# The head of a two-layer decoder kernel: other order of transfers, squares summed ahead of one product by ones, row factors multiplied partly on POOL

## The chip, the cores and the metric

One core of a Trainium2 chip runs the whole program. The metric is the time of one execution in microseconds (us), the median of several runs on the device.

## The reference

Two decoder layers over 512 tokens of width 1024, each of which also attends into 256 fixed memory tokens. What the change touches is only the beginning: the memory and the input are normed by their root mean square, and the memory is multiplied by the key and value weights of both layers.

```python
def rms_norm(x, g):
    xf = x.astype(jnp.float32)
    y = xf * lax.rsqrt(jnp.mean(xf * xf, axis=-1, keepdims=True) + EPS)
    return (y * g.astype(jnp.float32)).astype(x.dtype)

mem_n = rms_norm(mem, ln_mem)                 # 256 memory tokens
for layer in range(DEPTH):                    # two layers
    h = rms_norm(x, ln_mix[layer])
    mkv = mem_n @ w_mem_kv[layer]             # keys, then values, 256 columns each
    mem_k, mem_v = mkv[..., :MEM_W], mkv[..., MEM_W:]
    if layer < N_A_LAYERS:
        mix_out, mem_q = gated_deltanet_mixer(h, gdn_w_in[a], ...)   # begins with h @ w_in
    ...
```

## The kernel before, in words

All activations lie with the features on the 128 partitions. The input `x` has eight rows of tiles (k = 0 to 7, each 128 features by 512 tokens), the memory `mem` eight rows of 128 by 256. Products are made in three parts: each factor is split into a rounded high part and the rest (`whi` and `wlo` of a weight, `h` and `l` of `x`, `mh` and `ml` of `mem`), and high by high, low by high and high by low are summed in PSUM by `mm3`. The high part is an ACT copy (`copy`, L148), the rest a DVE subtraction (`split`, L161, or with a gain in it `split_gain`, L164).

The head of the program is `mem_and_norm` and `gates`. Its work in the order of the code:

- transfers, all issued by SP: gains, `mem` in four pieces with the first key weight in two halves between them, the second key weight, the constants, `x` in four pieces, the value weights, `wab`, and layer 1's key and value weights;
- the split of the eight rows of `mem`;
- `keys(0)`: two tiles of 24 matmuls each (PE, `pj<-mh,whi` and the like), without the norm's factor;
- `memory_stats` and `rstd_of`: the squares of `mem` on ACT (L151), summed by twos on DVE (`sq<-sq,sq`), and four products by a matrix of ones that sum over the partitions (`g<-sq,consts`); the factor `mr` from an ACT logarithm and an exponential (L142); the same with eight squares and four products for `x`, factor `xr`;
- `memory_columns`: `mr` as a column `mc`, by four small records on PE; `values(0)`, then `keys(1)` and `values(1)` (48 matmuls each);
- `norm()`: per row of `x`, DVE multiplies by the gain and by `xr` (L164, `x<-x,gains,xr`), ACT copies it to `h`, DVE subtracts to `l`;
- `gates`: eight products of `x`'s rows by `wab` (`pj<-x,wab`), their sum is copied by ACT to `ab`, and products by a constant matrix turn it (`g<-consts,ab`). The first projection `key(0)` of the next part begins directly behind the eight products on PE, and `g<-consts,ab` stands four matmuls into it.

Which engine does a step is written in the code. The order on each engine is set by a scheduler that works ahead of the run from priorities and estimates of its own; each engine then runs its list strictly in that order, and an instruction that waits holds up all behind it.

Of the kernel before, what the change touches and what calls it, by code (L numbers as in the profile page):

```python
# [9 lines left out]
F32 = mybir.dt.float32  # L10
# [3 lines left out]
ALU = mybir.AluOpType  # L14
# [4 lines left out]
P = 128  # L19
T = 512  # L20
D = 1024
KD = D // P
# [3 lines left out]
ML = 256  # L26
# [13 lines left out]
G_MIX, G_FFN, G_MEM, G_KV, G_FIN = (0, 8), (16, 24), 32, 40, 48  # L40
# [4 lines left out]

C_ID, C_U, C_ONE, C_CAUS, C_BAND = 0, 128, 256, 384, 512
C_SEL, C_INV, C_SIGN = 768, 780, 781
C_N = 782

# [19 lines left out]
def constants():  # L69
    c = np.zeros((P, C_N), np.float32)  # L70
    i = np.arange(P)
    c[:, C_ID:C_ID + P] = np.eye(P)
    c[:, C_U:C_U + P] = i[:, None] <= i[None, :]
    c[:, C_ONE:C_ONE + P] = 1.0
    c[:, C_CAUS:C_CAUS + P] = np.where(i[None, :] >= i[:, None], 0.0, NEG)
    c[:, C_BAND:C_BAND + P] = np.where(i[None, :] > i[:, None], 0.0, NEG)
    c[:, C_BAND + P:C_BAND + 2 * P] = np.where(i[None, :] <= i[:, None], 0.0, NEG)
    for e in range(12):
        c[e, C_SEL + e] = 1.0
        for j in range(1, 4):  # L80
            c[32 * j + e, C_SEL + e] = 1.0
    for p in range(P):
        if p % 64 < 16:
            c[p, C_INV] = INV_FREQ[p % 8]
            c[p, C_SIGN] = -1.0 if p % 64 < 8 else 1.0
    return c


class Builder:
# [138 lines left out]

    def rstd_of(self, tiles, pool, out, after=None):

        ps = self.bank("g")[:, :tiles[0].shape[1]]
        for k in range(0, KD, 2):
            two = []
            for x in tiles[k:k + 2]:
                sq = self.t(pool, [P, x.shape[1]], F32, "sq", 6)
                two.append(sq)
                ins = self.square(sq, x)
                if after is not None:
                    self.nosync(ins, after)
            self.tt(self.nc.vector, two[0], two[0], two[1], ALU.add)  # L240
            self.mm(ps, self.ones, two[0], k == 0, k == KD - 2)
        self.rsqrt(out, ps, D)


    def build(self):
# [32 lines left out]
    def load_constants(self, cp):  # L278
        nc, a = self.nc, self.a
# [6 lines left out]
        self.U = c[:, C_U:C_U + P]  # L286
        self.ones = c[:, C_ONE:C_ONE + P]
        self.caus = c[:, C_CAUS:C_CAUS + P]
        self.band = c[:, C_BAND:C_BAND + 2 * P]
        self.one = c[:, C_ONE:C_ONE + 1]  # L290
        v = self.t(cp, [P, 10], F32, "eps")
# [12 lines left out]
    def mem_and_norm(self, ep):  # L304
# [7 lines left out]
        early = lambda src: self.load(src, ep, 6)  # L312
        raw = [self.t(ep, [P, D], F32, "wraw", 6)]
        for k in range(0, KD, 2):
            nc.sync.dma_start(mem[:, k:k + 2, :], a["memT"][:, k:k + 2, :])
            if k < 4:
                s = slice(k // 2 * T, (k // 2 + 1) * T)
                nc.sync.dma_start(raw[0][:, s], a["wmk"][0, 0][:, s])
        raw += [early(a["wmk"][0, 1])]
        self.fetch_constants()  # L320
        for k in range(KD):
            self.split_gain(mem[:, k, :], self.gain(G_MEM, k), mh[:, k, :], ml[:, k, :])
        for k in range(0, KD, 2):
            nc.sync.dma_start(x[:, k:k + 2, :], a["xT"][:, k:k + 2, :])
        raw += [early(s) for s in (a["wmv"][0, 0], a["wmv"][0, 1])]
        wab = self.wab = self.t(ep, [P, KD, 32], F32, "wab")
        nc.gpsimd.memset(wab, 0.0)
        nc.sync.dma_start(wab[:, :, 0:12], a["wab"])
        raw += [early(s) for s in (a["wmk"][1, 0], a["wmk"][1, 1], a["wmv"][1, 0], a["wmv"][1, 1])]
        self.kept = {}  # L330
        mr = self.t(ep, [P, ML], F32, "mr")
        mc = self.t(ep, [P, 2], F32, "mc")
        xr = self.t(ep, [P, T], F32, "xr")
        mem_stats = lambda after: self.memory_stats(ep, mem, mr, after)

        def keys(layer):
            ps, ks = [], []
            for m in range(2):
                w = self.weight(None, nc.vector, raw[4 * layer + m], 1 if m + layer else 2)
                ps.append(self.bank("sc" if layer else "pj")[:, :ML])  # L340
                for k in range(KD):
                    self.mm3(ps[m], w, k, (mh[:, k, :], ml[:, k, :]), k == 0, k == KD - 1)
            if layer == 0:
                mem_stats(self.copied)
            for m in range(2):
# [26 lines left out]
        def norm():  # L372
            self.h, self.hx = [], [x[:, k, :] for k in range(KD)]
            for k in range(KD):
                self.h.append(self.pair(self.apool))
                xk = x[:, k, :]
                self.stt(xk, xk, self.gain(G_MIX[0], k), xr, ALU.mult, ALU.mult)
                self.split(xk, *self.h[k])

        self.memK = keys(0)  # L380
        self.rstd_of([x[:, k, :] for k in range(KD)], ep, xr)
        self.memory_columns(mr, mc)
        self.memV = values(0)
        keys(1)
        values(1)
        norm()

    def memory_stats(self, ep, mem, mr, after):
        self.rstd_of([mem[:, k, :] for k in range(KD)], ep, mr, after=after)

# [900 lines left out]
```

## Time and profile before

| what | value |
|---|---|
| median of 3 runs | 1148.49 us (1147.78 to 1148.76) |
| the profiled execution's own time | 1148.39 us |
| its span, first to last instruction | 1146.6 us |
| share of the span: PE, DVE, ACT, POOL | 98%, 73%, 55%, 7% |
| chain that ended last | PE 89%, DVE 5%, ACT 4%, DMA 1%, issue 1% |
| the eight products of the gates begin / end on PE | 40.53 us / about 42.4 us |

The head is the first 42 us of the span. In a row of the timeline the first number is the start, the second the duration (of all x instructions together), and in brackets stands how long the engine had been idle before, and what ended that. A row of a table by stages gives the stretch, its length, and for each engine the busy time and the number of instructions. In a row of groups the number behind the bar is the busy time of the group and then the mean duration of one instruction in ns.

### The profile page before, as it was taken

How to read it: one execution, taken by the hardware profiler on the slowest of the kernel's cores; microseconds unless marked ns; L12 is line 12 of the kernel's file. 1: busy time of each engine (PE TensorE's matmuls, PEld its weight loads, DVE VectorE, ACT ScalarE, POOL GpSimd, SP SyncE). 2: the span in 40 equal slices, each digit the busy share in tenths (PEclk: the TensorE clock that was granted, in tenths of full speed). 3: DMA queues.
4: the chain of work that ended last, by engine and by line, in shares of the span. 5: the costliest groups of instructions: out<-in, count | busy, mean ns of one | idle time of the engine just before them, and what ended most of it. 6: DMA issues, size and time to landing. Idle time of an engine off the chain costs nothing.

```text
span 1146.6 us, 19668 instructions
## 1 busy us (share of the span) xinstructions
PE 1127.0 (98%) x7476; PEld 990.7 (86%) x7476; DVE 841.2 (73%) x1587; ACT 631.5 (55%) x1271; POOL 86.0 (7%) x97
## 2 busy tenths in 40 slices
PE   7999999999999999999999999999999999999996
PEld 5888887887899998899998777778999988999986
DVE  5764887766789987489866777759699843898754
ACT  7579572366556652256654556765566522566533
POOL 0220000000101100011100000010011100111000
PEclk9999999999999999999999999999999999999999
DMA  8333342325657744567723411144477733577232
GB/s 312 124 116 108 123 107 97 99 86 166 175 142 190 189 125 125 151 151 182 184 74 101 138 56 56 56 111 129 105 191 188 187 108 106 141 191 185 70 96 93
DMA packets 73972, 152.83 MB, mean 133 GB/s; under 512 B 17757, under 2 KB 18421, under 8 KB 73877
## 3 DMA queue, kind: packets, MB, share of 16 engines
q1 hardware_dynamic: 62356, 130.59, 36.8%
q0 software_dynamic: 11520, 20.98, 11.6%
q8 instruction: 59, 0.97, 0.4%
q14 instruction: 37, 0.30, 0.1%
HBM read 144.58 MB, written 6.96 MB: 132 GB/s over the span
## 4 chain that ended last, share of the span: by engine, by line
PE 89%; DVE 5%; ACT 4%; DMA 1%; issue 1%; SPq 0%; DVEq 0%; ACTq 0%
PE pj L154 44%; PE g L154 38%; PE sc L154 6%; ACT sm L142 2%; DVE wlo L161 1%; PE g L158 1%; DMA wraw<-in_wmk 1%; DVE q L161 0%; DVE sm L784 0%; PE qk L154 0%; ACT sm L148 0%; DVE l L164 0%; ACT whi L148 0%; ACT pf L148 0%; DVE l L161 0%
## 5 line engine op out<-in xcount | busy, mean ns | idle before, releaser
L148 ACT ACTIVATE whi<-wraw 128x512 fp32r<-128x512 f32 (+2 forms) x331 | 243.9, 746 | 244.9 <-PE pj L154 151.8
L161 DVE TENSOR_TENSOR wlo<-wraw,whi 128x512 fp32r<-128x512 f32 (+2 forms) x331 | 274.8, 840 | 102.6 <-ACT whi L148 96.8
L154 PE MATMUL pj<-h,whi 128*128 128x512 f32 (+1 forms) x676 | 267.4, 397 | 0.2 <-ACT h L148 0.2
L154 PE MATMUL pj<-l,whi 128*128 128x512 f32 (+1 forms) x676 | 264.2, 391 | 0.6 <-DVE l L164 0.4
L154 PE MATMUL pj<-h,wlo 128*128 128x512 f32 (+1 forms) x676 | 264.0, 390 | 0.0
L154 PE MATMUL g<-T,whi 128*128 128x256 f32 x1280 | 228.1, 278 | 0.2
L154 PEld LDWEIGHTS g<-T,whi 128*128 128x128 f32 x1280 | 194.7, 188 | 1.8 <-DVE fu L164 1.8
L154 PE MATMUL g<-T,wlo 128*128 128x256 f32 x640 | 177.8, 278 | 0.0
L154 PEld LDWEIGHTS pj<-h,whi 128*128 128x128 f32 x676 | 126.8, 188 | 31.2 <-issue 5.8
L154 PEld LDWEIGHTS pj<-l,whi 128*128 128x128 f32 x676 | 127.1, 188 | 26.8 <-issue 1.1
L154 PEld LDWEIGHTS pj<-h,wlo 128*128 128x128 f32 x676 | 127.0, 188 | 25.7 <-issue 0.3
L154 PE MATMUL g<-h,whi 128*128 128x256 f32 (+1 forms) x508 | 144.5, 285 | 0.0
L154 PE MATMUL g<-h,wlo 128*128 128x256 f32 (+1 forms) x508 | 144.3, 284 | 0.0
L154 PE MATMUL g<-l,whi 128*128 128x256 f32 (+1 forms) x508 | 144.2, 284 | 0.0
L154 PEld LDWEIGHTS g<-T,wlo 128*128 128x128 f32 x640 | 120.1, 188 | 0.0
L154 PEld LDWEIGHTS g<-h,whi 128*128 128x128 f32 x508 | 95.3, 188 | 1.5 <-issue 0.3
L154 PEld LDWEIGHTS g<-l,whi 128*128 128x128 f32 x508 | 95.3, 188 | 1.2
L154 PEld LDWEIGHTS g<-h,wlo 128*128 128x128 f32 x508 | 95.3, 188 | 1.1
L1025 POOL DMA_DIRECT2D ws<-in_wgu x40 | 35.4, 885 | 693.6 <-DMA ws<-in_wgu 274.9
L148 ACT ACTIVATE whi<-ws 128x512 fp32r<-128x512 f32 x80 | 50.5, 631 | 49.0 <-PE g L154 40.2
L161 DVE TENSOR_TENSOR fu<-pj,rstd 128x512 f32<-128x512 f32 (+1 forms) x34 | 22.4, 660 | 54.5 <-PE pj L154 54.4
L161 DVE TENSOR_TENSOR wlo<-ws,whi 128x512 fp32r<-128x512 f32 x80 | 54.9, 686 | 6.4 <-ACT whi L148 6.3
(355 smaller groups left out, 1617.9 us busy)
## 6 DMA issues: line engine op xcount, KB each, us to landing
wraw<-in_wgu SPq DMA_DIRECT2D x48, 512.0 KB, 4.3
ws<-in_wgu SPq DMA_DIRECT2D x80, 256.0 KB, 3.5
ws<-in_wgu POOLq DMA_DIRECT2D x80, 256.0 KB, 4.8
wraw<-in_wdn SPq DMA_DIRECT2D x48, 384.0 KB, 3.1
wraw<-in_win SPq DMA_DIRECT2D x26, 512.0 KB, 3.6
wraw<-in_wgu SPq DMA_DIRECT2D x40, 256.0 KB, 4.2
wraw<-in_wout SPq DMA_DIRECT2D x16, 512.0 KB, 3.6
wraw<-in_wdn SPq DMA_DIRECT2D x16, 256.0 KB, 2.7
```

The lines of the kernel that those rows point to most:

```text
L142: ins = self.nc.scalar.activation(out, in_, func, **kw).ins
L148: self.copied = self.nc.scalar.activation(out, in_, AF.Copy, **kw).ins
L154: return self.nc.tensor.matmul(out, lhsT, rhs, start=start, stop=stop, skip_group_check=more).ins
L158: return self.nc.tensor.transpose(out, in_, self.ident[:k, :k]).ins
L161: return eng.tensor_tensor(out=out, in0=a, in1=b, op=op).ins
L1025: nc.gpsimd.dma_start(s1, a22, accum_op=ALU.add)
```

## The change

- Transfers: the second key weight is loaded in two halves, layer 0's value weights come ahead of `x`, and the constants come last. The matrix of ones is no longer among them: DVE fills it.
- Squares of `mem`: four POOL products of two rows each (128x512) in place of eight ACT squares; DVE adds them up, and there is one product by ones in place of four. Squares of `x`: four ACT instructions of two rows each in place of eight; DVE adds all of them up, and one product stands in place of four. That product moves into `keys(1)`, behind the first row.
- `norm()`: the factor `xr` alone is multiplied into the rows of `x`, on POOL for rows 0, 2, 4, 6 and 7 and on DVE for 1, 3 and 5 (tensor by tensor, without the gain). The gain goes into the ACT copy to `h` and into the DVE instruction that makes `l` (`split_gain`), and for the gates into `wab`, by one POOL instruction.

```diff
--- before.py
+++ after.py
@@ -43,9 +43,9 @@
 G_N = G_GDN + 1
 
 
-C_ID, C_U, C_ONE, C_CAUS, C_BAND = 0, 128, 256, 384, 512
-C_SEL, C_INV, C_SIGN = 768, 780, 781
-C_N = 782
+C_ID, C_U, C_CAUS, C_BAND = 0, 128, 256, 384
+C_SEL, C_INV, C_SIGN = 640, 652, 653
+C_N = 654
 
 
 INV_FREQ = [float.fromhex(s) for s in (
...
@@ -225,22 +224,6 @@
 
         self.fn(out, in_, AF.Ln, scale=1.0 / mean, bias=self.eps if eps is None else eps)
         self.fn(out, out, AF.Exp, scale=-0.5)
-
-    def rstd_of(self, tiles, pool, out, after=None):
-
-        ps = self.bank("g")[:, :tiles[0].shape[1]]
-        for k in range(0, KD, 2):
-            two = []
-            for x in tiles[k:k + 2]:
-                sq = self.t(pool, [P, x.shape[1]], F32, "sq", 6)
-                two.append(sq)
-                ins = self.square(sq, x)
-                if after is not None:
-                    self.nosync(ins, after)
-            self.tt(self.nc.vector, two[0], two[0], two[1], ALU.add)
-            self.mm(ps, self.ones, two[0], k == 0, k == KD - 2)
-        self.rsqrt(out, ps, D)
-
 
     def build(self):
         tc, nc, a = self.tc, self.nc, self.a
@@ -284,10 +267,11 @@
         self.consts, self.gains, self.small = c, g, s
         self.ident = c[:, C_ID:C_ID + P]
         self.U = c[:, C_U:C_U + P]
-        self.ones = c[:, C_ONE:C_ONE + P]
+        self.ones = self.t(cp, [P, P], F32, "ones")
+        nc.vector.memset(self.ones, 1.0)
         self.caus = c[:, C_CAUS:C_CAUS + P]
         self.band = c[:, C_BAND:C_BAND + 2 * P]
-        self.one = c[:, C_ONE:C_ONE + 1]
+        self.one = self.ones[:, 0:1]
         v = self.t(cp, [P, 10], F32, "eps")
         self.minuses = [v[:, 2 + 4 * i:6 + 4 * i] for i in range(2)]
         nc.vector.memset(v[:, 0:1], EPS)
@@ -310,38 +294,69 @@
         ml = self.t(ep, [P, KD, ML], F32R, "ml")
         self.use(LN_EXP)
         early = lambda src: self.load(src, ep, 6)
-        raw = [self.t(ep, [P, D], F32, "wraw", 6)]
+        raw = [self.t(ep, [P, D], F32, "wraw", 6) for _ in range(2)]
+        half = [slice(i * T, (i + 1) * T) for i in range(2)]
         for k in range(0, KD, 2):
             nc.sync.dma_start(mem[:, k:k + 2, :], a["memT"][:, k:k + 2, :])
             if k < 4:
-                s = slice(k // 2 * T, (k // 2 + 1) * T)
-                nc.sync.dma_start(raw[0][:, s], a["wmk"][0, 0][:, s])
-        raw += [early(a["wmk"][0, 1])]
-        self.fetch_constants()
+                nc.sync.dma_start(raw[0][:, half[k // 2]], a["wmk"][0, 0][:, half[k // 2]])
+        for s in half:
+            nc.sync.dma_start(raw[1][:, s], a["wmk"][0, 1][:, s])
+        raw += [early(s) for s in (a["wmv"][0, 0], a["wmv"][0, 1])]
         for k in range(KD):
             self.split_gain(mem[:, k, :], self.gain(G_MEM, k), mh[:, k, :], ml[:, k, :])
         for k in range(0, KD, 2):
             nc.sync.dma_start(x[:, k:k + 2, :], a["xT"][:, k:k + 2, :])
-        raw += [early(s) for s in (a["wmv"][0, 0], a["wmv"][0, 1])]
         wab = self.wab = self.t(ep, [P, KD, 32], F32, "wab")
         nc.gpsimd.memset(wab, 0.0)
         nc.sync.dma_start(wab[:, :, 0:12], a["wab"])
         raw += [early(s) for s in (a["wmk"][1, 0], a["wmk"][1, 1], a["wmv"][1, 0], a["wmv"][1, 1])]
+        self.fetch_constants()
         self.kept = {}
         mr = self.t(ep, [P, ML], F32, "mr")
         mc = self.t(ep, [P, 2], F32, "mc")
         xr = self.t(ep, [P, T], F32, "xr")
-        mem_stats = lambda after: self.memory_stats(ep, mem, mr, after)
-
-        def keys(layer):
+
+        def summed(pairs):
+            for i, j in ((0, 1), (2, 3), (0, 2)):
+                self.tt(nc.vector, pairs[i], pairs[i], pairs[j], ALU.add)
+            return pairs[0]
+
+        def squares_of_memory():
+            pairs = []
+            for k in range(0, KD, 2):
+                sq = self.t(ep, [P, 2, ML], F32, "mq", 4)
+                self.tt(nc.gpsimd, sq, mem[:, k:k + 2, :], mem[:, k:k + 2, :], ALU.mult)
+                pairs.append(sq)
+            both = summed(pairs)
+            self.tt(nc.vector, both[:, 0, :], both[:, 0, :], both[:, 1, :], ALU.add)
+            return both[:, 0, :]
+
+        def squares_of_x():
+            pairs = []
+            for k in range(0, KD, 2):
+                sq = self.t(ep, [P, 2, T], F32, "sq", 4)
+                self.square(sq, x[:, k:k + 2, :])
+                self.tt(nc.vector, sq[:, 0, :], sq[:, 0, :], sq[:, 1, :], ALU.add)
+                pairs.append(sq[:, 0, :])
+            return summed(pairs)
+
+        def rstd_of(sq, out):
+            ps = self.bank("g")[:, :sq.shape[1]]
+            self.mm(ps, self.ones, sq)
+            self.rsqrt(out, ps, D)
+
+        def keys(layer, between=None):
             ps, ks = [], []
             for m in range(2):
-                w = self.weight(None, nc.vector, raw[4 * layer + m], 1 if m + layer else 2)
+                w = self.weight(None, nc.vector, raw[4 * layer + m], 1 if layer else 2)
                 ps.append(self.bank("sc" if layer else "pj")[:, :ML])
                 for k in range(KD):
                     self.mm3(ps[m], w, k, (mh[:, k, :], ml[:, k, :]), k == 0, k == KD - 1)
+                    if between is not None and m == 0 and k == 3:
+                        between()
             if layer == 0:
-                mem_stats(self.copied)
+                rstd_of(squares_of_memory(), mr)
             for m in range(2):
                 kt = self.t(ep, [P, ML], F32, "kt", 2) if layer else self.t(self.mpool, [P, ML], F32, f"mk{m}")
                 self.tt(nc.vector, kt, ps[m], mr, ALU.mult)
@@ -371,22 +386,18 @@
 
         def norm():
             self.h, self.hx = [], [x[:, k, :] for k in range(KD)]
+            self.tt(nc.gpsimd, wab, wab, self.gains[:, G_MIX[0]:G_MIX[0] + KD].unsqueeze(2).to_broadcast([P, KD, 32]), ALU.mult)
             for k in range(KD):
                 self.h.append(self.pair(self.apool))
-                xk = x[:, k, :]
-                self.stt(xk, xk, self.gain(G_MIX[0], k), xr, ALU.mult, ALU.mult)
-                self.split(xk, *self.h[k])
+                self.tt(nc.vector if k in (1, 3, 5) else nc.gpsimd, x[:, k, :], x[:, k, :], xr, ALU.mult)
+                self.split_gain(x[:, k, :], self.gain(G_MIX[0], k), *self.h[k])
 
         self.memK = keys(0)
-        self.rstd_of([x[:, k, :] for k in range(KD)], ep, xr)
         self.memory_columns(mr, mc)
         self.memV = values(0)
-        keys(1)
+        keys(1, lambda: rstd_of(squares_of_x(), xr))
         values(1)
         norm()
-
-    def memory_stats(self, ep, mem, mr, after):
-        self.rstd_of([mem[:, k, :] for k in range(KD)], ep, mr, after=after)
 
     def memory_columns(self, mr, mc):
```

What the scheduler makes of it, by engine. Names carry buffer numbers: `mq` are the POOL squares of `mem`, `x` the eight rows of the input. POOL, from its clearing of `wab` on, before:

```order
L327 MEMSET wab_126 128x256
L671 MEMSET big_1312 96x1024
L687 MEMSET X_285_1414 128x1536
L672 MEMSET big_1312 96x32
L693 MEMSET Tt_1420 128x3072
L161 ISA
```

and now:

```order
L311 MEMSET wab_127 128x256
L160 ISA
L160 TENSOR_TENSOR mq_205<-mem_88 128x512
L160 TENSOR_TENSOR mq_207<-mem_88 128x512
L160 TENSOR_TENSOR mq_209<-mem_88 128x512
L160 TENSOR_TENSOR mq_211<-mem_88 128x512
L160 TENSOR_TENSOR wab_127<-wab_127,gains_67 128x256
L160 TENSOR_TENSOR x_89<-x_89,xr_142 128x512 x5
```

POOL had only clearing to do in the head; it now has ten computing instructions, four of them while `keys(0)` runs, and its setup instruction (`ISA`) has moved ahead of them.

DVE in the norm (`wlo` of a weight, `kt` layer 1's keys, rows of `x`, and `l`); before, from its third row on:

```order
L164 SCALAR_TENSOR_TENSOR x_87<-x_87,gains_67,xr_139 128x512
L161 TENSOR_TENSOR wlo_390<-wraw_133,whi_389 128x1024
L161 TENSOR_TENSOR kt_382<-sc_328,mr_137 128x256
L161 TENSOR_TENSOR l_465<-x_87,h_464 128x512
L161 TENSOR_TENSOR wlo_394<-wraw_135,whi_393 128x1024
L164 SCALAR_TENSOR_TENSOR x_87<-x_87,gains_67,xr_139 128x512
```

and now:

```order
L160 TENSOR_TENSOR wlo_376<-wraw_134,whi_375 128x1024
L160 TENSOR_TENSOR kt_368<-sc_295,mr_140 128x256
L160 TENSOR_TENSOR x_89<-x_89,xr_142 128x512
L160 TENSOR_TENSOR wlo_380<-wraw_136,whi_379 128x1024
L163 SCALAR_TENSOR_TENSOR l_442<-x_89,gains_67,h_441 128x512
L160 TENSOR_TENSOR kt_372<-sc_343,mr_140 128x256
L163 SCALAR_TENSOR_TENSOR l_447<-x_89,gains_67,h_446 128x512
L163 SCALAR_TENSOR_TENSOR l_452<-x_89,gains_67,h_451 128x512
L160 TENSOR_TENSOR x_89<-x_89,xr_142 128x512 x2
L160 TENSOR_TENSOR wlo_563<-wraw_560,whi_562 128x1024
L163 SCALAR_TENSOR_TENSOR l_457<-x_89,gains_67,h_456 128x512
```

DVE has three multiplications of rows in place of eight, and the last two of them (rows 3 and 5) stand behind `l` of rows 0, 1 and 2.

ACT from the second copy of layer 0's values (`mv`) through the logarithm and the exponential of `x`'s factor (`xr`), now:

```order
L147 ACTIVATE mv_43_289<-pj_264,mc_141 128x256
L147 ACTIVATE whi_291<-wraw_130 128x1024
L147 ACTIVATE whi_339<-wraw_132 128x1024
L141 ACTIVATE xr_142<-g_323,eps_72 128x512
L147 ACTIVATE whi_375<-wraw_134 128x1024
L141 ACTIVATE xr_142<-xr_142 128x512
```

The first `whi` of `keys(1)` now stands behind the copy of the second values; before, it stood ahead of the first one. Further on, this stands ahead of the copy `ab` on ACT now:

```order
L147 ACTIVATE h_456<-x_89,gains_67 128x512
L147 ACTIVATE kt_408<-sc_383,mc_141 128x256
L147 ACTIVATE h_461<-x_89,gains_67 128x512
L147 ACTIVATE h_466<-x_89,gains_67 128x512
L147 ACTIVATE h_471<-x_89,gains_67 128x512
L147 ACTIVATE h_476<-x_89,gains_67 128x512
L147 ACTIVATE kt_437<-pj_412,mc_141 128x256
L147 ACTIVATE whi_599<-wraw_597 128x1024
L147 ACTIVATE ab_490<-pj_481 128x512
```

The first of these, `h` of row 3, waits for DVE's row 3; before, two of the eight `h` and one copy stood directly ahead of `ab`, and the second projection's `whi` ahead of those.

On PE the product by ones for `mem` now stands behind five matmuls of `values(0)`, `mr`'s small records behind twenty, and the product for `x` behind two matmuls of `keys(1)`; before, all of these stood between `keys(0)` and `values(0)`.

1 line of the change is left out of this document (removed).

## The prediction

> **What bounds the kernel now.** First the page's busy times: PE works 98% of the span, so the change can only win where PE waits or does work that can go.
>
> ```profile
> span 1146.6 us, 19668 instructions
> PE 1127.0 (98%) x7476; PEld 990.7 (86%) x7476; DVE 841.2 (73%) x1587; ACT 631.5 (55%) x1271; POOL 86.0 (7%) x97
> ```
>
> Then the table by stages, cut where PE passes from one stage to the next: `keys(0)`, the products by ones, `values(0)`, `keys(1)`, `values(1)`, and from the gates on.
>
> ```profile
> core 0: us, PE busy (x) PEld busy (x) DVE busy (x) ACT busy (x) POOL busy (x), PEclk, DMA share, GB/s
> 6.92:15.91 8.99, 8.23 (x48) 7.78 (x49) 6.53 (x13) 7.78 (x19) 0.00 (x0) 1.00 0.99 376
> 15.91:22.01 6.10, 6.07 (x23) 3.23 (x22) 3.71 (x7) 5.02 (x11) 0.00 (x0) 1.00 1.05 367
> 22.01:28.92 6.91, 6.75 (x50) 6.10 (x49) 5.49 (x7) 5.57 (x8) 0.00 (x0) 1.00 0.75 304
> 28.92:34.68 5.76, 5.76 (x50) 5.76 (x49) 5.76 (x8) 3.35 (x5) 2.34 (x3) 1.00 0.07 24
> 34.68:40.53 5.85, 5.85 (x50) 5.72 (x48) 5.85 (x10) 4.49 (x7) 0.03 (x1) 1.00 0.13 46
> 40.53:48.08 7.55, 7.55 (x46) 4.98 (x45) 4.73 (x10) 3.27 (x8) 2.66 (x1) 1.00 0.54 158
> ```
>
> Two things are to be seen. The 48 matmuls of `keys(1)` take 5.76 us, 0.12 each; the same number in `keys(0)` takes 8.99, in `values(0)` 6.91, and 6.10 go to products by ones. So the head holds some 10 us that aren't main products. And from 28.92 to 40.53 DVE has no idle time at all (5.76 of 5.76, 5.85 of 5.85): PE finds its operands there only just in time.
>
> The timeline gives PE's pieces: the fourth column is the line, x is the count.
>
> ```profile
> 9.74 0.41 PE L154 MATMUL pj<-mh,wlo 128*128 128x256 f32 x1
> 11.57 0.28 PE L154 MATMUL pj<-mh,wlo 128*128 128x256 f32 x1
> 12.05 0.36 PE L154 MATMUL pj<-mh,whi 128*128 128x256 f32 x1
> 10.91 1.06 ACT L148 ACTIVATE whi<-wraw 128x1024 fp32r<-128x1024 f32 x1 [0.40 <-DMA wraw<-in_wmk]
> 13.28 0.19 PEld L154 LDWEIGHTS pj<-mh,wlo 128*128 128x128 f32 x1 [0.96 <-DVE wlo L161]
> 16.03 3.83 PE L154 MATMUL g<-sq,consts 128*128 128x256 f32 x12
> 17.75 1.02 PE L154 MATMUL g<-sq,consts 128*128 128x512 f32 x2
> ```
>
> Each product by ones is two records. The eight of `mem` start from 16.03 to 17.75: 0.215 a record, 0.43 a product; those of `x`, twice as wide, 0.86. The second key tile begins at 12.05, and after two matmuls PE waits 0.96 for that weight's `wlo`, which is late because its transfer ends at 10.9. That is the only wait of the head's matmuls that goes back to a DMA.
>
> **POOL and DVE side by side.** The change puts nine POOL instructions with two tensors in SBUF into a stretch in which DVE is busy with the same kind. The head before has no such pair; further on there are two. POOL's `DT` rows (about 1.25 us each) run here against DVE's `wlo`:
>
> ```profile
> L161 POOL TENSOR_TENSOR DT<-gcr,consts 128x512 f32<-128x512 f32 x6 | 8.5, 1457 | 9.5 <-DMA gcr<-dr 9.5
> 57.29 2.30 POOL L161 TENSOR_TENSOR DT<-gcr,consts 128x512 f32<-128x512 f32 x1
> 62.05 1.28 POOL L161 TENSOR_TENSOR DT<-gcr,consts 128x512 f32<-128x512 f32 x1
> L161 DVE TENSOR_TENSOR wlo<-wraw,whi 128x1024 fp32r<-128x1024 f32 x9 | 11.0, 1224 | 2.7 <-ACT whi L148 2.6
> 56.38 2.05 DVE L161 TENSOR_TENSOR wlo<-wraw,whi 128x1024 fp32r<-128x1024 f32 x1 [0.66 <-ACT whi L148]
> 58.35 2.30 DVE L164 SCALAR_TENSOR_TENSOR kn<-pj,gains,kn 128x511 f32<-128x511 f32 x3
> 62.38 2.04 DVE L161 TENSOR_TENSOR wlo<-wraw,whi 128x1024 fp32r<-128x1024 f32 x1 [1.72 <-ACT whi L148]
> ```
>
> A `wlo` alone takes 1.22. The one at 56.38 comes in the middle of a `DT` and takes 2.05, as if it stood still for 0.82 until that one was over (57.2); the `DT` at 57.29 then takes 2.30 in place of 1.28 and ends 1.15 behind that `wlo`. The `wlo` at 62.38 comes 0.33 into a `DT` of 1.28 and again takes 0.82 more. The three `kn` from 58.35 on, with one operand in PSUM, keep their 0.75 beside POOL. So I read: a DVE instruction with two SBUF operands and a POOL instruction that reads SBUF exclude each other, whole instructions at a time, and at a boundary the one that waits goes next. The Trainium skill says so too ("SBUF — State Buffer", section "SBUF: two separate sides"): the two engines share a pair of ports, given as an exclusive lock for a whole instruction. The trace agrees, with its 0.82 and its 2.30. Without that page the four rows alone carry the sum.
>
> **The change part by part.** Made against the profiled execution's 1148.39 us, 0.10 below the median of 1148.49. Durations overlap their successor by some 0.08, so spacings are used: the pair of `ml` below takes 0.88, 0.40 + 0.48.
>
> ```profile
> 5.45 0.91 ACT L148 ACTIVATE mh<-mem,gains 128x256 fp32r<-128x256 f32 x2 [3.43 <-DMA mem<-in_memT]
> 5.99 0.88 DVE L164 SCALAR_TENSOR_TENSOR ml<-mem,gains,mh 128x256 fp32r<-128x256 f32 x2 [3.08 <-ACT mh L148]
> L161 DVE TENSOR_TENSOR wlo<-wraw,whi 128x512 fp32r<-128x512 f32 x2 | 1.4, 692 | 0.1
> 42.68 2.66 POOL L693 MEMSET Tt<- 128x3072 f32 x1 [7.96 <-issue]
> L148 ACT ACTIVATE h<-x 128x512 fp32r<-128x512 f32 x8 | 4.7, 622 | 1.1 <-DVE x L164 1.1
> L148 ACT ACTIVATE whi<-wraw 128x1024 fp32r<-128x1024 f32 x10 | 10.5, 1054 | 3.2 <-PE sc L154 1.8 <-PE pj L154 0.9 <-DMA wraw<-in_wmk 0.4
> L148 ACT ACTIVATE mv<-pj,mc 128x256 f32<-128x256 f32 x2 | 0.9, 466 | 0.2 <-PE pj L154 0.2
> L142 ACT ACTIVATE xr<-g,eps 128x512 f32<-128x512 f32 x1 | 0.7, 688 | 0.9 <-PE g L154 0.9
> L142 ACT ACTIVATE xr<-xr 128x512 f32<-128x512 f32 x1 | 0.6, 618 | 0.0
> L148 ACT ACTIVATE ab<-pj 128x512 f32<-128x512 f32 x1 | 0.6, 598 | 1.0 <-PE pj L154 1.0
> 40.53 1.92 PE L154 MATMUL pj<-x,wab 128*32 128x512 f32 x16
> wraw<-in_wmv SPq DMA_DIRECT2D x4, 512.0 KB, 7.8
> consts<-in_consts SPq DMA_DIRECT2D x1, 391.0 KB, 7.3
> ```
>
> *Transfers.* The second key weight in halves would remove the wait of 0.96. The order of the rest is worth nothing: no other transfer is waited for, two value weights ahead of `x` in place of the constants (1024 KB for 391) delay `x` by 0.65 MB at 0.37 MB/us, 1.7 us, while its squares are wanted later than before. The constants come last but are wanted first by `g<-consts,ab`. DVE's filling of the ones lies ahead of its first `ml` at 5.99, where it is idle.
>
> *`keys(0)`.* PE's first tile needs eight `ml` and two half `wlo`: 8 x 0.40 + 2 x 0.61 = 4.4 us of DVE. POOL's four squares, 4 x 1.25 = 5.0, want the same port. From 5.99 on that is 15.4 if all four squares get in between, and PE ends the tile at about 15.8; before, it did so at 12.0. When POOL begins is not shown: its setup instruction can have cost anything from 0 to the 9.4 us between the end of `Tt` (45.34) and the first `DT` (54.80). Begun at once, when the first piece of `mem` has landed (5.4), POOL has half an instruction done ahead of DVE, and the tile ends at 15.2; begun after 10.5, the tile is on time, but DVE's adding of `mq` stands ahead of the second tile's `wlo` and waits for POOL, and the second tile ends at 19.8. I take the middle. The Trainium skill has about 6 us for a first call ("GPSIMD Engine Reference", section "2.1 Instruction dispatch"), by which POOL would begin at about 7.1 and the tile would end at 15.8; no run here shows it. The second tile is then 24 x 0.12 = 2.9 and about 0.6 of waiting for its first `wlo` behind `mq`: end at 19.3 (18.7 to 19.8) against 15.91. **+3.4** (+2.8 to +3.9).
>
> *Products by ones.* The stage of 6.10 goes: **-6.1**. In `values(0)` come 0.43 for the one product and about 0.4 for `mr`'s four records. Waits there before: 6.91 - 5.76 = 1.15. After: about 0.7 for `wlo` of the value weights, late behind `mq`, and at the end 0.47 + 1.05 for `mv` and the `whi` of `keys(1)`, which now follow each other on ACT after the last matmul. 5.76 + 0.83 + 0.7 + 1.5 = 8.8: **+1.9**. In `keys(1)` 0.86 for `x`'s product and some 0.2 of waiting: **+1.05**. Up to here 3.4 - 6.1 + 1.9 + 1.05 = **+0.25**; `values(1)` ends at 40.8.
>
> *The rows of `x`.* `keys(1)` begins at 28.2, its product by ones ends at 29.3, and ACT then does logarithm, a `whi` and exponential (0.69 + 0.96 + 0.62, with gaps): `xr` at 31.7. From there the port carries five POOL rows, 6.25, and on DVE up to row 5: the rest of a `wlo` 0.6, row 1 0.6, a `wlo` 1.15, three `l` 2.0, rows 3 and 5 1.2, together 5.55. 31.7 + 11.8 = 43.5, and the gates begin at 43.7 in place of 40.8: **+2.9**. Side by side they would be ready by 38, and POOL's part would cost nothing.
>
> *`ab`.* The gates end at 45.6. On ACT five `h` (0.53 apart, from row 3's 43.2 on), two copies and a `whi` stand ahead of `ab`: 2.65 + 0.75 + 0.96, then 0.60, so 48.2. PE meets `g<-consts,ab` four matmuls of 0.23 after the gates, at 46.5: **+1.7**.
>
> Later stages move along; nothing there changes kind. Sum +4.85 with POOL's squares begun at about 7, +4.2 with POOL at once. I take +4.5: **1152.9 us**, 0.4% slower.
>
> **Rivals.**
> *Side by side (faster).* If POOL's rows and DVE's do not exclude each other: `keys(0)` -1.0 (the wait of 0.96), -6.1, +1.7, +1.05, the rest nothing: -4.4, or 1144.0; with POOL late, at 10.5, -2.2. Against it stand the two `wlo` of 2.05; for it only that two meetings are few, and that with `mq` and `x` none is seen.
> *Only tensor-by-tensor (no change).* The meetings show a `wlo` (TENSOR_TENSOR). `ml` and `l` multiply by a gain too (SCALAR_TENSOR_TENSOR), and none of these with two SBUF operands meets POOL in the trace. If they pass, `keys(0)` is +1.0, and the rows of `x` cost about 1 in place of 4.6: 1.0 - 6.1 + 1.7 + 1.05 + 1.0 + about 0.8 for `ab` = -0.5, or 1147.9, within -2 to +3 by POOL's beginning.
> *PE's clock.* PE's spacing is 0.21 at 9.74 (duration 0.41) and 0.12 from 11.45 on (0.28). If the slow pace is left only after some time of dense work, a first tile full of waits keeps it for the second tile: 24 x 0.09 = +2.2 on top, 1155.1.
>
> **How the numbers follow.** Exclusion as read 60 in 100 (10 of it with the clock), only tensor-by-tensor 14, side by side 26. Own range of the likeliest 1150.8 to 1155.5. To hold 8 in 10 the range reaches into side by side: 1144.0 (half of that case lies above, by POOL's late beginning) to 1155.5. A measurement tells about 0.2% (2.3 us) from no change: exclusion gives slower 56 and same 4, tensor-by-tensor faster 3, same 7, slower 4, side by side faster 25, same 1.
>
> **What would show it.** Right: POOL's `mq` and `x` rows with durations of 1.9 to 2.5 or `ml` and `l` of 1.2 to 2 beside them; `keys(0)` ending after 18; the gates waiting for DVE or POOL; `ab` late. The 6.10 gone in any case. Wrong: `ml` at 0.48 and POOL at 1.28 in the same microseconds, `values(0)` beginning near 15.

## The result, and the profile after

The changed kernel takes 1153.19 us (median of 4 runs, 1152.51 to 1155.06) against 1148.13 us of the kernel before beside it: a ratio of 1.0047 (95% interval 1.0029 to 1.0064), so it is slower by about 0.5%. The forecast was 1152.9. The profiled execution took 1152.51 us, 4.12 more than the one before. The total came out as worked out; its parts did not, as the following rows show.

The table by stages of the kernel after: `keys(0)`, `values(0)`, `keys(1)`, `values(1)`, the gates, and from about the first projection to the product by `gate`. The table of before had a row for the products by ones, and the last two of these in one row.

```profile
core 0: us, PE busy (x) PEld busy (x) DVE busy (x) ACT busy (x) POOL busy (x), PEclk, DMA share, GB/s
6.94:18.46 11.52, 10.44 (x49) 9.51 (x50) 11.28 (x17) 7.13 (x12) 3.42 (x3) 1.00 1.06 394
18.46:27.03 8.57, 7.06 (x56) 6.66 (x54) 5.67 (x10) 5.86 (x10) 0.75 (x1) 1.00 0.79 308
27.03:34.10 7.07, 7.06 (x50) 6.21 (x51) 6.43 (x7) 5.45 (x7) 3.36 (x2) 1.00 0.15 33
34.10:39.95 5.85, 5.85 (x50) 5.72 (x48) 5.85 (x5) 1.77 (x3) 5.85 (x5) 1.00 0.26 96
39.95:43.10 3.15, 3.04 (x18) 0.84 (x18) 3.15 (x5) 2.00 (x4) 0.86 (x1) 1.00 0.01 4
43.10:52.60 9.50, 7.19 (x27) 5.30 (x28) 6.14 (x12) 5.04 (x10) 4.04 (x3) 0.82 0.58 165
```

The stage of products by ones is gone, `keys(0)` has grown by 2.5, and the last row holds what was not foreseen: 2.3 us without PE work and a granted clock of 0.82 (column PEclk, as a share of PE's full clock).

POOL and DVE in the timeline, the squares of `mem` first, then the rows of `x`:

```profile
5.44 1.04 POOL L160 TENSOR_TENSOR mq<-mem 128x512 f32<-128x512 f32 x1 [4.39 <-DMA mem<-in_memT]
7.47 3.55 POOL L160 TENSOR_TENSOR mq<-mem 128x512 f32<-128x512 f32 x3 [0.98 <-DMA mem<-in_memT]
30.74 9.18 POOL L160 TENSOR_TENSOR x<-x,xr 128x512 f32<-128x512 f32 x5 [10.77 <-ACT xr L141]
6.00 1.16 DVE L163 SCALAR_TENSOR_TENSOR ml<-mem,gains,mh 128x256 fp32r<-128x256 f32 x2 [3.10 <-ACT mh L147]
7.96 2.16 DVE L163 SCALAR_TENSOR_TENSOR ml<-mem,gains,mh 128x256 fp32r<-128x256 f32 x2 [0.20 <-ACT mh L147]
10.04 1.52 DVE L160 TENSOR_TENSOR wlo<-wraw,whi 128x512 fp32r<-128x512 f32 x1
11.49 1.66 DVE L163 SCALAR_TENSOR_TENSOR ml<-mem,gains,mh 128x256 fp32r<-128x256 f32 x4
33.04 2.31 DVE L160 TENSOR_TENSOR wlo<-wraw,whi 128x1024 fp32r<-128x1024 f32 x1
37.33 3.14 DVE L163 SCALAR_TENSOR_TENSOR l<-x,gains,h 128x512 fp32r<-128x512 f32 x2
40.39 1.28 DVE L160 TENSOR_TENSOR x<-x,xr 128x512 f32<-128x512 f32 x2
```

POOL begins the moment the first piece of `mem` lands. Its first square, begun ahead of DVE's first `ml`, takes 1.04. Beside POOL two `ml` take 1.16 and then 2.16 in place of 0.88, a half `wlo` 1.52 in place of 0.69, a whole one 2.31 in place of 1.22, two `l` 3.14 in place of about 1.4; POOL's five rows of `x` take 1.84 each. The last `ml` ends at 13.15, with POOL done.

PE at the end of `keys(0)`, at the gates and at `ab`, and below them what ACT does ahead of `ab`:

```profile
12.02 0.58 PE L153 MATMUL pj<-ml,whi 128*128 128x256 f32 x1 [0.83 <-DVE ml L163]
14.53 0.41 PE L153 MATMUL pj<-mh,whi 128*128 128x256 f32 x1
16.66 0.41 PE L153 MATMUL pj<-ml,whi 128*128 128x256 f32 x1
17.38 0.28 PE L153 MATMUL pj<-mh,whi 128*128 128x256 f32 x1
39.95 3.07 PE L153 MATMUL pj<-x,wab 128*32 128x512 f32 x16
46.48 1.06 PE L153 MATMUL g<-consts,ab 128*128 128x12 f32 x8 [2.31 <-ACT ab L147]
48.16 0.63 PE L153 MATMUL pj<-h,whi 128*128 128x512 f32 x1
48.59 0.63 PE L153 MATMUL pj<-l,whi 128*128 128x512 f32 x1
42.09 2.55 ACT L147 ACTIVATE h<-x,gains 128x512 fp32r<-128x512 f32 x4
44.90 1.05 ACT L147 ACTIVATE whi<-wraw 128x1024 fp32r<-128x1024 f32 x1
45.84 0.58 ACT L147 ACTIVATE ab<-pj 128x512 f32<-128x512 f32 x1
```

The second key tile begins at 14.53. The key matmuls go at the slow pace (0.21 apart, 0.41 long) until 16.9; before, they did so until 11.4. The column PEclk reads 1.00 there in both kernels: so early in the span the spacing tells the pace, not the column. After the wait for `ab` the projections stand 0.43 apart in place of 0.23, and here the column shows it too:

```profile
46.48:47.66 1.18, 1.18 (x9) 1.18 (x10) 0.77 (x1) 0.00 (x0) 1.18 (x2) 1.00 0.09 23
47.66:51.07 3.41, 3.41 (x9) 2.65 (x9) 1.53 (x3) 1.34 (x3) 1.48 (x1) 0.50 0.54 158
51.07:55.00 3.93, 3.93 (x20) 2.87 (x19) 0.90 (x6) 1.51 (x6) 0.00 (x0) 1.00 0.47 137
```

Put together, where PE passes in the two profiled executions:

| point on PE | before | after | later by | predicted |
|---|---|---|---|---|
| `keys(0)` ends | 15.91 | 18.46 | +2.55 | +3.4 |
| `values(0)` begins | 22.01 | 18.46 | -3.55 | -2.7 |
| `keys(1)` begins | 28.92 | 27.03 | -1.89 | -0.8 |
| gates begin | 40.53 | 39.95 | -0.58 | +3.2 |
| first projection | 42.39 | 42.96 | +0.57 | +3.2 |
| `g<-consts,ab` | 43.42 | 46.48 | +3.06 | +4.8 |
| `g<-consts,gate` | 48.08 | 52.60 | +4.52 | +4.8 |
| whole execution | 1148.39 | 1152.51 | +4.12 | +4.5 |

Of the 4.5 at `g<-consts,gate` 4.1 are left at the end. At one place further on PE waited 0.62 for `N` in the profiled execution before, and not in the one after; at that place the distance is 4.08. The repeat of the changed kernel, further down, waited 0.60 there, and among the other kernels the wait is anything from nothing to 0.88, so it is the executions that differ there and not the kernels.

```profile
266.11 3.03 PE L154 MATMUL g<-N,consts 128*128 128x512 f32 x6 [0.62 <-DVE N L161]
270.19 3.03 PE L153 MATMUL g<-N,ones 128*128 128x512 f32 x6
```

### The profile page after: what moved, and what is told of

Its sections match the earlier page's. It is cut to its first block, busy times and chain, and to the rows that moved or that the text cites. A ratio compares the mean times of both kernels' runs of the same rounds, so it can differ in the third digit from the quotient of the medians.

```text
span 1150.6 us, 19646 instructions
## 1 busy us (share of the span) xinstructions
PE 1127.4 (98%) x7464; PEld 991.7 (86%) x7464; DVE 846.0 (74%) x1587; ACT 629.5 (55%) x1260; POOL 100.5 (9%) x107
## 4 chain that ended last, share of the span: by engine, by line
PE 88%; DVE 5%; ACT 4%; issue 1%; DMA 0%; SPq 0%; DVEq 0%; ACTq 0%
PE pj L153 44%; PE g L153 38%; PE sc L153 5%; ACT sm L141 2%; DVE wlo L160 1%; DVE l L163 1%; PE g L157 1%; ACT whi L147 1%; DVE q L160 0%; DVE sm L795 0%; DMA mem<-in_memT 0%; PE qk L153 0%; ACT sm L147 0%; ACT h L147 0%; ACT pf L147 0%
```

## The experiments

Three theories were put against each other. **Exclusion**: POOL and DVE keep each other from SBUF, whole instructions at a time, and the change pays for that in `keys(0)`, in the rows of `x` and in the late `ab`. **Clock**: the loss is PE's slow pace, kept longer at the start and come back after `ab`. **Side by side**: the two engines don't hinder each other, and the loss comes from the new order. Times are medians; ratios are to the kernel before run beside each. Remarks behind a # in the edits are added for the reader.

| kernel | us | before | ratio, 95% interval |
|---|---|---|---|
| after, again | 1154.12 | 1148.09 | 1.0049 (1.0037 to 1.0062) |
| rows of `x` all on DVE | 1149.48 | 1147.68 | 1.0015 (1.0007 to 1.0024) |
| squares of `mem` on ACT | 1149.38 | 1147.68 | 1.0014 (1.0005 to 1.0024) |
| both | 1146.04 | 1147.68 | 0.9984 (0.9975 to 0.9993) |
| PE warmed ahead | 1153.69 | 1147.68 | 1.0048 (1.0036 to 1.0061) |
| PE warmed and filled in `keys(0)` | 1153.29 | 1147.91 | 1.0044 (1.0031 to 1.0057) |
| PE filled in the wait for `ab` | 1152.51 | 1147.91 | 1.0040 (1.0027 to 1.0053) |
| before, POOL reads beside DVE | 1151.86 | 1147.91 | 1.0035 (1.0023 to 1.0046) |
| before, POOL fills beside DVE | 1148.07 | 1147.91 | 1.0000 (0.9991 to 1.0009) |
| before, only the transfers | 1146.45 | 1148.09 | 0.9984 (0.9976 to 0.9993) |
| squares on ACT, `ab` ahead | 1146.27 | 1148.19 | 0.9986 (0.9977 to 0.9995) |
| both, PE warmed | 1145.67 | 1148.09 | 0.9976 (0.9966 to 0.9986) |

**Do POOL and DVE exclude each other?** Two kernels of before with work on POOL that nothing waits for.

```diff
+            junk = self.t(ep, [P, T], F32, "junk")          # POOL reads
+            for _ in range(6):
+                self.tt(nc.gpsimd, junk, xr, xr, ALU.mult)
```
```diff
+            junk = self.t(ep, [P, 3 * T], F32, "junk")      # POOL fills
+            self.tt(nc.gpsimd, junk[:, :T], xr, xr, ALU.mult)
+            for _ in range(5):
+                nc.gpsimd.memset(junk, 0.0)
```

> The kernel before, with six more POOL products of 128x512 (xr by xr into a tile that nothing reads), started when xr is ready; no instruction waits for them, so they can cost time only by being there. Exclusion: POOL's six take 7.5 us alone and 10 to 11 beside DVE, which is full from 28.9 to 40.5; each DVE instruction with two SBUF operands in that stretch gets 0.8 to 1.1 longer, six to eight of them, so 4 to 6 us later at the gates: 1152 to 1154, with x and l rows of 1.3 to 1.8 in place of 0.7. Only tensor by tensor (rival): the rows here are the form with a gain (SCALAR_TENSOR_TENSOR), which then pass at 0.7; only three or four wlo and kt are hit: +1 to +2. Side by side: 1147.7, no change.

> Control for the one before: one such product on POOL when xr is ready, and behind it five fillings with zero of a tile of 128x1536 (1.38 us each by the row of X), so POOL is busy for some 8 us in the same stretch, but reads no SBUF in most of it. Exclusion of readers of two operands: +0 to +1.3 (the one product), 1147.7 to 1149.0. If any POOL work on SBUF locks DVE out, as much as the one before: 1152 to 1154. Side by side: 1147.7.

The timeline of the first, from the end of `xr` on, and then of the second:

```profile
25.93 8.22 POOL L161 TENSOR_TENSOR junk<-xr 128x512 f32<-128x512 f32 x5
28.30 1.53 DVE L161 TENSOR_TENSOR l<-x,h 128x512 fp32r<-128x512 f32 x1
29.75 1.52 DVE L164 SCALAR_TENSOR_TENSOR x<-x,gains,xr 128x512 f32<-128x512 f32 x1
31.20 2.06 DVE L161 TENSOR_TENSOR wlo<-wraw,whi 128x1024 fp32r<-128x1024 f32 x1
34.63 0.74 DVE L164 SCALAR_TENSOR_TENSOR x<-x,gains,xr 128x512 f32<-128x512 f32 x1
```
```profile
26.17 7.15 POOL L377 MEMSET junk<- 128x1536 f32 x5
27.71 0.68 DVE L161 TENSOR_TENSOR l<-x,h 128x512 fp32r<-128x512 f32 x1
28.32 0.74 DVE L164 SCALAR_TENSOR_TENSOR x<-x,gains,xr 128x512 f32<-128x512 f32 x1
28.98 1.21 DVE L161 TENSOR_TENSOR wlo<-wraw,whi 128x1024 fp32r<-128x1024 f32 x1
```

Beside POOL's reading products every DVE instruction with two SBUF operands gets about 0.8 longer, with a gain in it (1.52) as well as without (1.53), and goes back to 0.74 once POOL has ended. The addition is the same for a `wlo` of twice the size (2.06 in place of 1.21), so it is a turn that DVE waits out and not a share of its speed that it loses. POOL's own products take 1.64 on average, where the first square of `mem`, also one tile by itself, took 1.04. That costs 3.9 us of time though nothing waits for the result. A stretch of fillings nearly as long (7.15 in place of 8.22) changes neither the rows beside it nor the time. So the exclusion is shown, for both forms of DVE instruction, and it is between readers: the rivals "side by side" and "only tensor-by-tensor" fall. The Trainium skill ("SBUF — State Buffer", section "SBUF: two separate sides") gives the lock for a DVE instruction with two SBUF inputs only against a GpSimd one that reads SBUF; both pairs agree.

**What each use of POOL costs.** The rows back to DVE, the squares to ACT, and both:

```diff
-                self.tt(nc.vector if k in (1, 3, 5) else nc.gpsimd, x[:, k, :], x[:, k, :], xr, ALU.mult)
+                self.tt(nc.vector, x[:, k, :], x[:, k, :], xr, ALU.mult)
```
```diff
-            pairs = []
+            pairs, last = [], self.copied
...
-                self.tt(nc.gpsimd, sq, mem[:, k:k + 2, :], mem[:, k:k + 2, :], ALU.mult)
+                self.nosync(self.square(sq, mem[:, k:k + 2, :]), last)
```

> After, with all eight rows of x multiplied by their factor on DVE; POOL keeps the four squares and the factor on the gate weights. Exclusion: the five rows on POOL (1.84 us each, 9.18 in all) and DVE's rows, wlo and l beside them take the port in turns; eight rows on DVE at about 0.6 each are shorter than that. l back at about 0.5, the gates are fed without waits, ab comes some 2 us earlier on ACT (43.8 in place of 45.84): 1150.5 to 1151.5, and if the stretch at half clock behind the wait for ab goes with that wait, 1149 to 1150. keys(0) is unchanged and still ends at 18.5. Clock alone (rival): the rows cost nothing, only the wait that drops the clock does; then 1151.5 if the wait goes, 1153 if not. Side by side (rival): POOL's five rows were free, and five more rows of 0.6 on the full DVE delay the gates by 2 to 3: 1155 to 1156.

> After, with the four squares of mem made by ACT (each of two tiles of 128x256, behind the last copy of mem's rows); POOL keeps the five rows of x. Exclusion: ml back to about 0.45 each and wlo to 0.7, the first key tile ends at about 12.2 and keys(0) at about 16 in place of 18.46; nothing behind it gives that back, so 1150 to 1151, the rows and the late ab staying. Clock (rival): with a dense first tile the full clock comes at about 11.5 in place of 16.9, which is 1.4 us of those 2.5; a gain of 1.4 alone would be 1151.8. Side by side (rival): POOL's squares cost nothing, ACT's four squares of some 0.65 delay the copies of the key and value weights by 2.6: 1153 to 1155.

> Both of the two before: squares of mem on ACT and all rows of x on DVE; on POOL stays only the factor on the gate weights. What is left of the change is the order of the transfers, the second key weight in halves, one product by ones in place of four and the gain moved. Exclusion: the two gains add up, 1146.5 to 1148, that is 0.5 to 2 us below the kernel before, with values(0) beginning at about 16.3, the gates at about 38.5 and no drop of the clock. Clock alone: 1149.5 to 1151.5. Side by side: 1154 to 1157.

Against the change (1.0047) the first gives back 0.32%, 3.7 us, the second 0.33%, 3.8 us, and both together 0.63%, 7.2 us. Within the intervals, some 1 us for each of these kernels and 2 us for the change, the two costs add up, and neither needs the other. With the squares on ACT, `ml` is back at its duration and `keys(0)` ends at 15.35, 3.1 earlier than after. But 3.6 ahead of after at the gates, that kernel met the wait for `ab` too, and in its profiled execution, the slowest of its eleven (1151.18), twice as long a stretch at half clock behind it:

```profile
5.95 0.88 DVE L163 SCALAR_TENSOR_TENSOR ml<-mem,gains,mh 128x256 fp32r<-128x256 f32 x2 [3.09 <-ACT mh L147]
42.92 1.67 PE L153 MATMUL g<-consts,ab 128*128 128x12 f32 x8 [2.30 <-ACT ab L147]
43.20:50.02 6.82, 6.82 (x21) 5.66 (x21) 2.49 (x7) 1.71 (x4) 2.39 (x1) 0.50 0.46 144
```

Its eleven executions give a price for the second half of that stretch. The mean clock was 0.994 in the profiled one and in two more, and these three took 1150.8 on average; the other eight, at 0.996 or 0.997, took 1149.3. The difference is 1.6, if 0.994 means two pieces in all three.

**Is it the rows on POOL, or the place of `ab`?** The same kernel with ACT's copy of `ab` moved ahead of the last two `h` and of a `whi`:

```diff
+                self.behind = [*getattr(self, "behind", []), self.copied]   # the copies to h
...
         self.copy(ab, ps)
+        for i in self.behind[-2:]:
+            self.nosync(i, self.copied)
+        self.held, self.ab_copy = 0, self.copied      # the second weight's copy waits too
```

> The kernel with ACT's squares of mem (POOL keeps the five rows of x; 1149.38, 1.4 above before), with ACT's copy of ab put ahead of the last two h and of the second projection's whi. Nothing is computed differently. There PE waited 2.30 for ab and then went 6.8 us at half clock (16 projections of 0.43 in place of 0.23). If that wait and the drop behind it are the price of POOL's rows, ab comes at about 40.7 in place of 42.9, PE waits under 0.5, the clock stays: 1.9 for the wait and about 3 for the clock (in the profiled run; 1.5 in those with one stretch), less about 1 for the two h and the whi that now come later: 1145.5 to 1147. If POOL's rows cost by DVE's later l instead, the projections wait for l and h: 1148.5 to 1149.5.

ACT and PE there, and the clock:

```profile
39.88 0.59 ACT L147 ACTIVATE ab<-pj 128x512 f32<-128x512 f32 x1
40.52 1.06 PE L153 MATMUL g<-consts,ab 128*128 128x12 f32 x8
42.00:46.00 4.00, 4.00 (x19) 3.30 (x18) 2.58 (x5) 2.29 (x4) 2.13 (x1) 1.00 0.28 88
```

`ab` comes 2.4 earlier, PE does not wait for it, the clock stays, and the ratio falls from 1.0014 to 0.9986: 3.2 us. That is nearly all of the 3.4 that the rows on POOL cost with the squares on ACT (1.0014 against 0.9984). The exclusion by itself costs PE nothing at the rows. With all rows on DVE (squares on ACT in both) the last gate product waits for DVE, and PE comes to `g<-consts,ab` at 41.68, behind five projections; here it comes there at 40.52, behind four:

```profile
39.95 1.05 PE L153 MATMUL pj<-x,wab 128*32 128x512 f32 x2 [0.30 <-DVE x L160]
41.68 1.06 PE L153 MATMUL g<-consts,ab 128*128 128x12 f32 x8
```

What costs is where `ab` comes to stand when the rows end together and late. With the squares on POOL too, as in the change, this edit was not run; there the same wait of 2.3 is read from the trace.

**How much of it is the clock?** Products that nothing reads keep PE busy: ahead of the first key matmul; there and between the rows of the first key tile; in the wait for `ab`.

```diff
+        warm = self.bank("g")
+        for _ in range(13):
+            self.mm(warm[:, :P], self.ones, self.ones)
...
+                    for _ in range(2 if layer == m == 0 and k < KD - 1 else 0):     # second kernel
+                        self.nosync(self.mm(warm[:, :P], self.ones, self.ones), self.last)
```
```diff
+        for _ in range(15):                                          # third kernel, alone
+            self.nosync(self.mm(pt[:, P:2 * P], self.ones, self.ones), self.copied)
```

> After, with 13 products of the ones by the ones (128x128, f32, not used by anything) put ahead of PE's first key product, in time in which PE has nothing to do (1.0 to 6.9 us). Clock theory: PE reaches the full clock before the first key product, so that key matmuls stand 0.12 apart from 6.94 on. The first key tile is held by ml and wlo anyway, but the second, and the 15 matmuls at the slow pace from 14.5 on, gain 15 x 0.09 = 1.4: keys(0) ends at about 17, 1151.5 to 1152. If the clock falls again in the waits of the first tile, it gains nothing: 1153. Exclusion alone, with the slow pace only a result of a start-up time that no work shortens: 1153 as well.

> After, with the 13 products ahead of the first key product and two more such products after each of the first seven rows of the first key tile, where PE waits for ml and wlo (0.215 each at full clock, read by nothing). Clock theory: PE has no idle stretch any more, the full clock comes before 7 us and stays; the first tile ends with its last ml at about 13.5 in place of 14.5, the second tile goes at 0.12: keys(0) ends at 16.5 to 17 in place of 18.46. DVE's wlo for the value weights then comes next at 17.4, so of the 1.5 to 2 some 1 stays: 1152. If the waits and not the clock set the end of keys(0): 18.3 to 18.9 and 1153 to 1153.5.

> After, with 15 products of ones by ones (128x128, f32, 3.2 us in all, read by nothing) on PE in the wait for ab; they stand after the first product of the projection, so three of its products (0.7 us) move behind ab. Clock theory: the stretch at half clock behind that wait (47.66 to 51.07, about 1.5 us of cost) goes, less the 0.7: 0.5 to 1.2 faster than after, so 1152 to 1152.7. If the drop is not set by PE's idle time: no drop removed, +0.7: 1153.9.

The stages of the first, then a stretch of the second:

```profile
7.17:10.44 3.27, 1.74 (x10) 1.32 (x10) 3.27 (x4) 3.27 (x8) 3.14 (x3) 1.00 1.04 405
10.44:17.28 6.84, 6.38 (x29) 5.79 (x28) 6.80 (x12) 3.74 (x5) 0.47 (x1) 0.50 1.04 403
47.44:57.68 10.24, 10.24 (x30) 7.80 (x30) 1.72 (x9) 3.14 (x8) 0.66 (x1) 0.50 0.32 115
```

Warmed ahead, PE began its key matmuls at 0.12 apart, was busy 1.74 of 3.27 us because it waited for `ml` and `wlo`, and was put to half clock at 10.44: `keys(0)` ended at 18.73, as late as without. With fillers in the waits too it kept full clock through `keys(0)`, but the fillers held the first tile up until 14.9, and `keys(0)` ended at 17.99 to 18.3; in its profiled execution the drop after `ab` then lasted 10.24. So the slow pace in `keys(0)` follows from the waits, and neither set of fillers took its cost away: the first let the clock fall in the waits, the second cost PE as much time itself. What the slow pace alone costs there was not measured. The third kernel kept full clock through the wait, but its order changed too:

```profile
43.26 3.51 PE L153 MATMUL g<-ones 128*128 128x128 f32 x30
50.69 0.40 PE L153 MATMUL g<-consts,gate 128*24 128x128 f32 x2 [1.18 <-DVE gate L163]
```

Three projections moved behind `ab`, and PE came to `gate` behind 9 projections in place of 20, too early, and waited 1.18. Its ratio, 1.0040, cannot be told from 1.0047. So that the wait brings the drop is shown (filled, no drop; removed, no drop), while the drop's price is read from the trace: from 47.74 to 51.12 eight spacings of 0.42 in place of 0.23, 1.5 us.

**The rest of the change.** Before with the transfers alone, and the kernel without POOL warmed:

```diff
-        raw = [self.t(ep, [P, D], F32, "wraw", 6)]
+        raw = [self.t(ep, [P, D], F32, "wraw", 6) for _ in range(2)]
...
+        raw += [early(s) for s in (a["wmv"][0, 0], a["wmv"][0, 1])]   # ahead of x; constants last
...
-                w = self.weight(None, nc.vector, raw[4 * layer + m], 1 if m + layer else 2)
+                w = self.weight(None, nc.vector, raw[4 * layer + m], 1 if layer else 2)
```

> The kernel before with only the order of the transfers, the ones filled on DVE and the second key weight brought and split in halves; squares, products by ones and the rows of x stay as before. By the prediction this removes the wait of 0.96 ahead of the second key tile and nothing else: 1146.8 to 1147.3, if DVE, full from 28.9 on, lets it through, 1147.8 if it does not. Rival: the later x (1.7 us) or the constants, wanted first by the product for ab, make a new wait: 1148 to 1149.

> The kernel without POOL's squares and rows (1146.04 before), and the 13 products of ones by ones ahead of the first key product. There the first key tile has few waits, so the full clock should hold: the tile goes at the pace of ml (0.45 a row), not 0.64, and ends at about 11.7 in place of 12.3; the second at 14.7. Then wlo of the value weight, which ended at 16.2 behind mq, sets the start of values(0) all the same: 1145.6 to 1146.1. If the slow pace at the start had been on the path: 1144.7 to 1145.3. If PE's idle stretches drop the clock again: 1146.5 to 1147.5.

The transfers alone, with the ones filled by DVE, are worth 1.8 us (0.8 to 2.8): the wait of 0.96 ahead of the second key tile is gone, and the only new wait of PE's matmuls in the head is one of 0.16 for `gate`. What else makes up the 1.8 was not taken apart. It is as much as the whole change without POOL gains (0.9984 both), so the sums, the single products and the moved gain bring nothing that can be told, within some 1.5 us either way. PE does win by them at first: without POOL it begins `values(0)` 6.8 earlier than before. At the gates 3.9 are left, at `g<-consts,gate` 2.3.

```profile
36.60:45.77 9.17, 8.68 (x44) 4.66 (x43) 6.86 (x13) 4.40 (x10) 4.05 (x3) 1.00 0.36 119
24.17 0.62 ACT L142 ACTIVATE xr<-xr 128x512 f32<-128x512 f32 x1
26.69 0.62 ACT L141 ACTIVATE xr<-xr 128x512 f32<-128x512 f32 x1
```

The first row is that kernel's stage from the gates to `gate`, 9.17 where before took 7.55; the others are the end of `xr` before and without POOL. With all squares added first and one product in `keys(1)`, `xr` comes 2.5 later, and from there DVE's list (eight rows, eight `l`, four `wlo`) sets when the gates can end. Warming ends `keys(0)` 1.2 earlier (14.05 in place of 15.22), but then PE waits 1.14 for a `wlo` of the value weights. In the time it brings nothing certain (0.9976 against 0.9984, intervals overlapping); by its median this version is the fastest of all: 0.24% below before, 0.7% below the change.

The repeat of the changed kernel:

> The changed kernel once more, beside the two others and the kernel before on one chip, for more runs of it. As before: a ratio of 1.0047, 1152.7 to 1153.5. The granted clock of each run tells how long the stretch behind the wait for ab lasts: 0.997 where it is one piece of 3.4 us, 0.994 where it is two; if these are the slower runs, by some 1.5 us a piece, the spread of the changed kernel (1152.51 to 1155.06) is that of the clock; if clock and time do not go together, it is not.

It took 1153.2 to 1154.89. Clock and time go together only loosely: means of 0.996 at 1153.2 and 1154.0, of 0.994 at 1154.12 and 1154.3, 0.995 at the slowest. So not all of the spread of this kernel is the clock's; where the rest comes from is open.

## Why the prediction was right in the sum and wrong in its parts

- **POOL and DVE.** The reading of the four rows (whole instructions, taking turns) held, also for the form that those rows did not show. POOL began at once, the lower of the two bounds: its `mq` starts at 5.44 as `mem` lands. POOL's idle time ahead of it, 4.39, ended with the transfer. The figure of about 6 us that the Trainium skill has for a first call ("GPSIMD Engine Reference", section "2.1 Instruction dispatch") is not seen here.
- **`keys(0)`, +3.4 (2.8 to 3.9).** Measured +2.55, below the lower bound. The step that failed is the price of POOL's squares: I put all four on DVE's list at 1.25 each, 5.0 in all, and with POOL at once half a square less. They cost DVE 2.4 (0.28 on the first two `ml`, 1.28 on the next two, 0.83 on a half `wlo`): over half of the first square was done ahead of DVE, and the others held it for 0.5 to 0.8 each. So the last `ml` ended at 13.15 where the sum had 15.4. Part of this was lost again to the third rival, the slow pace. It held through the end of the first tile, which PE left only at 14.5, and into the second, which took 3.9 in place of 3.5: eleven matmuls by 0.09 make 1.0, while the 0.6 of waiting for `wlo` did not come.
- **Stage of products, -6.1; `values(0)`, +1.9; `keys(1)`, +1.05.** Measured -6.1, +1.66, +1.31: right on PE. What the sum did not say is that PE's lead is worth only what the engine that bounds the next stage leaves of it.
- **Rows of `x`, +2.9 at the gates.** Measured at the first projection +0.57 in place of +3.2. Three steps were too long. `xr` was ready at 30.66 and not at 31.7 (1.0), mostly because `keys(0)` had ended earlier. From there to the end of DVE's last row, at 41.67, the rows took 11.0 and not 11.8 (0.8). And I let the gates begin when the last row was ready: they began 0.58 earlier than before and worked through the rows as they came, 3.01 from first gate to first projection in place of 1.86, so that the first projection came 1.3 behind the last row and not 2.1 (0.8).
- **`ab`, +1.7.** Measured +2.5 from the first projection to `g<-consts,ab`, a wait of 2.31 in it. The queue ahead of it on ACT was named rightly (`h`, two copies, a `whi`).
- **"Later stages move along".** Wrong by 1.5: that wait brought PE to half clock for 3.41 us. I had put the clock at the start of the head alone.
- **The rival "side by side", 1144.0.** Without POOL there is no contention to pay, and the change gives 1.8 and not 4.4. That is not quite the rival's case, for all eight rows are DVE's there; but PE's lead over before shrinks from 6.8 at `values(0)` to 2.3 at `gate` behind DVE's list, which its "the rest nothing" left out.

The errors: -0.85 in `keys(0)` and about -1.8 at the rows, +0.8 at `ab` and +1.5 behind it. They nearly cancel, and the sum had no reason for that: that the total came out so near is luck. What the prediction had right by its reasons is that POOL and DVE would take turns, and that this and the late `ab` would cost more than the change saves.

## What to carry to other kernels

POOL is no spare DVE: beside POOL instructions of 128x512 that read SBUF, a DVE instruction with two SBUF operands that met them got 0.3 to 1.1 us longer here, unless it had begun first, while fillings cost it nothing; hand work to it only where DVE has time or reads PSUM. PE time removed ahead of a stage is a gain only if the chain into that stage (here squares, `xr`, DVE's rows, ACT's `ab`) comes as much earlier, so follow the vector engines' list and not PE's before counting it. A PE wait can cost more than its length: the one of 2.31 us here brought another 1.5 us by the clock, so look for what can go ahead of it in another engine's queue.

## What was not expected of the hardware

- The half-clock stretches last 3.41 us (after), 6.82 and 6.84 (squares on ACT; PE warmed) and 10.24 (PE filled in `keys(0)`): one, two and three times 3.41. The Trainium skill ("TensorE: Matmul & The Clock Gate", section "Part 1: The HAM clock gate") gives a free-running window of 3413 ns; the lengths agree.
- What it takes to fall is less than an idle window: after a single wait of 2.31, and in the warmed kernel with no wait longer than 1.21 but only 1.74 of 3.27 us busy. The same page (section "HAM oscillation — how this bites in real kernels") has as its rule no idle gaps over about 3.4 us; here shorter ones were enough. Not every one was: the wait of 1.51 ahead of `keys(1)` in the kernel after brought no fall, and the matmuls behind it stand 0.12 apart.
- Five fillings of 128x1536 on POOL, 1.43 us each, leave DVE's durations beside them as they are (0.68, 0.74, 1.21).
